# One level of Strassen's algorithm in the feed forward stages of a two-layer grid encoder

## The chip, the core and the metric
The kernel runs on one core of a Trainium2 chip as one program. The metric is the device time of one execution in microseconds. TensorE multiplies matrices, VectorE (DVE) and ScalarE (ACT) do the elementwise work, GpSimd (POOL) a part of it, and SyncE (SP) issues all the transfers of weights and activations discussed here.

## The reference
Two groups of tokens (512 prompt, 256 sample) go through the same weights, 768 tokens of width 1024 in all. Two layers, each a half-weighted feed forward, a mixer, and another half-weighted feed forward; a final norm ends it. The hidden width is 2752. The kernel's stages are therefore f, ab, f, f, c, f.
```python
def _rmsnorm(x, g):
    y = xf * lax.rsqrt(jnp.mean(xf * xf, axis=-1, keepdims=True) + NORM_EPS)
    return (y * g.astype(jnp.float32)).astype(x.dtype)
def _swiglu(h, wg, wu, wd):
    return (jax.nn.silu(h @ wg) * (h @ wu)) @ wd
...
        x = x + 0.5 * _swiglu(_rmsnorm(x, norm_ffn1[i]), ffn1_wg[i], ffn1_wu[i], ffn1_wd[i])
        h = _rmsnorm(x, norm_mix[i])
        ...
        x = x + 0.5 * _swiglu(_rmsnorm(x, norm_ffn2[i]), ffn2_wg[i], ffn2_wu[i], ffn2_wd[i])
    return _rmsnorm(x, final_norm)
```
The mixers (neighbourhood and latent attention in the first, grouped attention in the second) are not touched but for their output product.

## The kernel before
The residual stream `x` lies transposed in SBUF, 8 tiles of 128 features by 768 tokens. All products keep float32 accuracy by splitting both operands into a high part (a cast to fp32r, ScalarE) and a low part (the difference, VectorE), and by three passes: high with high, high with low, low with high. `mm3` (L163) issues these as six matmuls, one of 512 and one of 256 columns per pass.

`Weights` is a stream of weight units: SP loads a unit of 512 KB into a `raw` buffer (L149), ScalarE casts it (L161), VectorE subtracts (L162). A few units are prepared ahead of their use.

`ffn_body` walks the 21.5 hidden tiles in chunks of three (`FCH`). For a tile, `up` computes gate and up products (8 k-tiles each) into two PSUM buffers; `act` applies the row scale `rr` (1 / rms of each token, L378 and L380), silu on ScalarE (L379), the product (L388), and the split of the result (L389 on POOL, L390 on VectorE). The result stays in SBUF. `down` multiplies the chunk's activations by their rows of the down weights and adds each of the 8 output tiles to `x` (L416). Down products of one chunk stand between the up products of the next. After the last chunk each finished tile of `x` is spread into the next product's operand by `spread` (`h_hi` L247, `h_lo` L248) and squared (L258, L260). `rstd_cols` (L270 and on) and `rstd_rows` make the next norm's scale, while TensorE already works on the unscaled products. In the last feed forward `down_final` (L453) takes the final chunk a third of the tokens at a time.

Each engine executes its own list in a fixed order; the tile scheduler sets it when the program is built. `x` stays in SBUF through a whole feed forward. Before a mixer it is written to DRAM (`xscr`, L1555) and read back at its output product (L1503).

## Time and profile before
| quantity | value |
|---|---|
| time, median of 3 runs | 3011.42 us (3008.15 to 3012.95) |
| span of the profiled execution | 3010.3 us |
| PE busy | 2923.2 us, 97% |
| DVE busy | 1419.8 us, 47% |
| ACT busy | 867.8 us, 29% |
| POOL busy | 435.6 us, 14% |
| read from and written to DRAM | 218.14 MB, 55.77 MB |

The span runs from the first to the last instruction of the profiled execution. Busy time says how much of it an engine had work; it says nothing of who waited for whom. For this the chain of waits is read, which follows the last instruction back to what released it, step by step. A busy PE may still run at a lowered clock, so the granted clock of a stretch stands beside it.

### The profile page before, as it was taken

To read this page: it belongs to the slowest core of one execution; us is meant where nothing else is said; L and a number is where in the kernel's file an instruction comes from. 1 tells how busy PE (TensorE), PEld (TensorE's weight loads), DVE (VectorE), ACT (ScalarE), POOL (GpSimd) and SP (SyncE) were. 2 spreads that over 40 slices of the span, in tenths; PEclk is the share of its full clock that TensorE was granted. 3 is DMA by queue.
4 is the path that set the end of the run, shared out by engine and by line. 5 is a ranking of instruction groups with operands and counts; after the bars stand their busy time and mean duration, and the time that the engine had idled before them with its cause. 6 is when DMAs were issued, how large, how long until landed. Compare 5 with 4: busy or idle time off the path is not lost.

```text
span 3010.3 us, 42066 instructions
## 1 busy us (share of the span) xinstructions
PE 2923.2 (97%) x17562; PEld 2581.6 (86%) x17562; DVE 1419.8 (47%) x1876; ACT 867.8 (29%) x1431; POOL 435.6 (14%) x543
## 2 busy tenths in 40 slices
...
GB/s 134 64 99 93 80 63 75 83 140 255 248 241 89 71 66 62 63 62 64 77 51 62 64 64 63 63 71 88 101 117 159 129 91 63 63 64 63 64 57 50
DMA packets 314653, 276.63 MB, mean 92 GB/s; under 512 B 25888, under 2 KB 285152, under 8 KB 313440
## 3 DMA queue, kind: packets, MB, share of 16 engines
...
HBM read 218.14 MB, written 55.77 MB: 91 GB/s over the span
## 4 chain that ended last, share of the span: by engine, by line
PE 88%; DMA 5%; DVE 3%; issue 1%; ACT 1%; POOL 1%; SPq 0%; DVEq 0%; ACTq 0%; POOLq 0%
PE ps L172 73%; PE pj L525 2%; PE pj L529 2%; PE pj L528 2%; PE s L660 2%; DMA oscr<-of 1%; PE pc L918 1%; DMA mq<-mst 1%; DVE h_lo L248 1%; PE t L698 1%; PE ps L453 1%; DVE x L416 1%; PE o L720 1%; PE ps L358 1%; PE o L719 1%
## 5 line engine op out<-in xcount | busy, mean ns | idle before, releaser
L172 PE MATMUL ps<-h_hi,gul 128*128 128x512 f32 (+1 forms) x2720 | 700.4, 338 | 0.0
L172 PE MATMUL ps<-h_hi,guh 128*128 128x512 f32 (+1 forms) x2720 | 697.1, 337 | 0.0
L172 PE MATMUL ps<-h_lo,guh 128*128 128x512 f32 (+1 forms) x2720 | 696.6, 337 | 0.0
L161 ACT CAST guh<-raw 128x1024 fp32r<-128x1024 f32 (+3 forms) x224 | 232.8, 1041 | 1380.1 <-PE ps L172 1353.9
L172 PE MATMUL ps<-act,dnh 128*128 128x512 f32 (+1 forms) x2720 | 580.7, 337 | 0.0
L172 PEld LDWEIGHTS ps<-h_hi,guh 128*128 128x128 f32 x2720 | 417.2, 188 | 62.8 <-issue 0.7
L172 PEld LDWEIGHTS ps<-h_hi,gul 128*128 128x128 f32 x2720 | 416.1, 188 | 59.1
L172 PEld LDWEIGHTS ps<-h_lo,guh 128*128 128x128 f32 x2720 | 414.8, 188 | 60.2
L172 PEld LDWEIGHTS ps<-act,dnh 128*128 128x128 f32 x2720 | 416.3, 188 | 58.1
L416 DVE SCALAR_TENSOR_TENSOR x<-ps,x 128x768 f32<-128x768 f32 x248 | 234.8, 955 | 342.7 <-PE ps L172 342.6
L389 POOL TENSOR_SCALAR act<-upp 128x768 fp32r<-128x768 f32 x88 | 73.7, 837 | 1949.6 <-DVE upp L388 1639.9
L172 PE MATMUL ps<-act,dnl 128*128 128x512 f32 (+1 forms) x1296 | 331.0, 336 | 0.0
L162 DVE TENSOR_TENSOR gul<-raw,guh 128x1024 fp32r<-128x1024 f32 (+3 forms) x224 | 271.6, 1215 | 31.9 <-ACT guh L161 31.2
L380 DVE TENSOR_TENSOR upp<-ps,rr 128x768 f32<-128x768 f32 x84 | 80.4, 957 | 363.7 <-PE ps L172 363.5
L378 DVE TENSOR_TENSOR gate<-ps,rr 128x768 f32<-128x768 f32 x84 | 80.4, 958 | 300.7 <-PE ps L172 289.5
L172 PEld LDWEIGHTS ps<-act,dnl 128*128 128x128 f32 x1296 | 197.5, 188 | 27.6
L162 DVE TENSOR_TENSOR dnl<-raw,dnh 128x1024 fp32r<-128x1024 f32 x84 | 103.6, 1235 | 150.7 <-ACT dnh L161 150.7
L161 ACT CAST dnh<-raw 128x1024 fp32r<-128x1024 f32 x84 | 88.1, 1049 | 289.8 <-DMA raw<-in_ffn_wd_dram 201.8
L525 PE MATMUL pj<-guh,h_hi 128*128 128x256 f32 x576 | 168.2, 292 | 0.9 <-ACT h_hi L247 0.7
L529 PE MATMUL pj<-guh,h_lo 128*128 128x256 f32 x576 | 165.9, 288 | 0.6 <-DVE h_lo L248 0.6
L528 PE MATMUL pj<-gul,h_hi 128*128 128x256 f32 x576 | 164.8, 286 | 0.0
L646 POOL TENSOR_SCALAR p<-p,sm 128x256 f32<-128x256 f32 (+1 forms) x192 | 117.6, 625 | 138.3 <-DVE sm L643 112.2
...
## 6 DMA issues: line engine op xcount, KB each, us to landing
...
mq<-mst SPq DMA_DIRECT2D x24, 384.0 KB
...
xscr<-x SPq DMA_DIRECT2D x16, 384.0 KB
naq<-stage SPq DMA_DIRECT2D x16, 384.0 KB
```

Source lines behind the costliest of these rows:

```text
L161: nc.scalar.copy(out=h, in_=r)
L162: nc.vector.tensor_tensor(out=l, in0=r, in1=f32(h), op=ALU.subtract)
L172: mm = nc.tensor.matmul(out[:, s], w, x[:, s], start=start and n == 0, stop=stop and n == len(pairs) - 1)
L378: nc.vector.tensor_tensor(out=g, in0=pss[0][:, :T], in1=rr, op=ALU.mult)
L380: nc.vector.tensor_tensor(out=u, in0=pss[1][:, :T], in1=rr, op=ALU.mult)
L389: nc.gpsimd.tensor_scalar(out=a[:rows, 0], in0=u[:rows], scalar1=1.0, scalar2=1.0, op0=ALU.mult, op1=ALU.mult)
L416: nc.vector.scalar_tensor_tensor(out=x[:, j], in0=ps[:, :T], scalar=0.5, in1=x[:, j], op0=ALU.mult, op1=ALU.add)
L525: m = nc.tensor.matmul(out, self.h[:, k, s], wh[:, c], start=k == 0, stop=False)
L528: nc.tensor.matmul(out, self.h[:, k, s], wl[:, c], start=False, stop=False)
L529: nc.tensor.matmul(out, self.l[:, k, s], wh[:, c], start=False, stop=k == KT - 1)
L646: nc.gpsimd.tensor_scalar(out=pt[:, c], in0=pt[:, c], scalar1=sm[:, 2 + s:3 + s], scalar2=1.0, op0=ALU.mult, op1=ALU.mult)
L660: self.anchor = nc.tensor.matmul(ps[:, a:b], sa, mo, start=m == 0, stop=m == len(movs) - 1).ins
```

## The change
The feed forward is cut into two phases, and in both of them a product of two matrices, each divided into 2 by 2 blocks, is computed by seven block products for eight (Strassen's algorithm in Winograd's form, one level), with sums and differences of blocks before and after.

Up, 20 of the 21.5 hidden tiles: the stationary matrix has two rows of blocks (gate, up) and two columns (the halves of the input features, 4 k-tiles each), the moving matrix has the two halves of the features by two halves of 384 tokens (`TH`, `HALVES`). `norm_half` scales a token half of x in advance (gain and row scale in one operation) and splits it; `combine` makes the four sums t1 to t4 of x's blocks, once for a feed forward. The weight sums are made per hidden tile by four operations of 128x512 (`sums` in `plan_up`); the units of a tile are ua (gate), ud (second half of up, 512 columns), uc (the sums) and ub (up). A block product is 4 k-tiles x 3 passes = 12 matmuls of 384 columns, so a tile takes 84. The finished activations, and for each pair of tiles the four combinations of them, go to DRAM (`tq`). The tile and a half left over are computed as before, in halves.

Down: groups of four hidden tiles, 5 of them; products are taken in the order `DOWN`, all five groups of one product in a row, each group 24 matmuls. The weights come as blocks of 128x1024 (two transfers), two of the four blocks (A and C) stay in SBUF, and the block sums are made in them by VectorE. The activations of a group come back from DRAM (`plan_acts`), are cast and subtracted. x, which was written to `xscr` and released, is loaded again, and the results of a product are added to it (L640). The tile and a half left over is multiplied for the first token half (`rest(0)`) between products 7 and 3, and for the second at the end.

Also, the mixers' output product runs in token halves, so that the next feed forward's `norm_half(0)` can start before its end.
```diff
+TH = T // 2
+HALVES = (slice(0, TH), slice(TH, T))
...
+    def norm_half(self, q, ps, gain):
+        nc = self.nc
+        rr = self.rstd_rows(q, ps)
+        x = self.xn[q]
+        for j in range(KT):
+            nc.vector.scalar_tensor_tensor(out=x[:, j], in0=self.x[:, j, HALVES[q]], scalar=gain[:, j:j + 1], in1=rr,
+                                           op0=ALU.mult, op1=ALU.mult)
+            if j % 2:
+                n, m = f"b{j // 4 + 1}{q + 1}", j % 4
+                hi, lo = (t[:, m - 1:m + 1] for t in self.comb[n])
+                nc.scalar.copy(out=hi, in_=x[:, j - 1:j + 1])
+                nc.vector.tensor_tensor(out=lo, in0=x[:, j - 1:j + 1], in1=f32(hi), op=ALU.subtract)
+    def combine(self, n, out, a, b):
+        nc = self.nc
+        nc.vector.tensor_tensor(out=out, in0=a, in1=b, op=ALU.subtract)
+        hi, lo = self.comb[n]
+        nc.scalar.copy(out=hi, in_=out)
+        nc.vector.tensor_tensor(out=lo, in0=out, in1=f32(hi), op=ALU.subtract)
...
+    NS = 20
+    OPS = {1: "b11", 2: "b21", 3: "b22", 4: "t4", 5: "t1", 6: "t2", 7: "t3"}
...
+    def plan_up(self, F, t, views):
+        nc = self.nc
+        st = []
+        def sums():
+            g, u = st
+            H = 512
+            tt = nc.vector.tensor_tensor
+            tt(out=u[:, H:], in0=u[:, :H], in1=u[:, H:], op=ALU.add)
+            tt(out=u[:, :H], in0=g[:, :H], in1=u[:, :H], op=ALU.subtract)
+            tt(out=g[:, :H], in0=u[:, H:], in1=g[:, :H], op=ALU.subtract)
+            tt(out=g[:, H:], in0=g[:, H:], in1=g[:, :H], op=ALU.subtract)
+            return self.split(g)
+        def load():
+            g = self.load_weight(views[0], P, 1024)
+            if t == 0:
+                st.extend((g, self.load_weight(views[1], P, 1024)))
+                return
+            u = F.evac.tile([P, 1024], F32, tag="rawu", name="rawu", bufs=2)
+            for view, src in views[1](u):
+                nc.sync.dma_start(out=view, in_=src)
+            st.extend((g, u))
+        self.gu.entry(load, lambda _: self.split(st[0]))
+        self.gu.entry(lambda: None, lambda _: self.split(st[1][:, 512:], 512))
+        self.gu.entry(lambda: None, lambda _: sums())
+        self.gu.entry(lambda: None, lambda _: self.split(st[1]))
+    DOWN = (1, 4, 5, 2, 6, 7, 0, 3)
...
+    def load_block(self, tile, F, q, a, b):
+        for m, src in enumerate(self.down_block(F.wd, q, a, b)):
+            self.nc.sync.dma_start(out=tile[:, 512 * m:512 * m + 512], in_=src)
+        return tile
+    def plan_down(self, F, i, q):
+        nc = self.nc
+        tt = nc.vector.tensor_tensor
+        new = lambda: self.wp.tile([P, 1024], F32, tag="raw", name="raw")
+        def stash(which, a, b):
+            t = F.stash.tile([P, 1024], F32, name=f"{which}{q}")
+            getattr(F, which)[q] = self.load_block(t, F, q, a, b)
+            return t
+        def s1(raw):
+            A, C = F.A[q], F.C[q]
+            tt(out=C, in0=raw, in1=C, op=ALU.add)
+            u = self.split(C)
+            tt(out=C, in0=C, in1=A, op=ALU.subtract)
+            tt(out=A, in0=A, in1=raw, op=ALU.subtract)
+            return u
+        def s4(raw):
+            tt(out=raw, in0=raw, in1=F.C[q], op=ALU.subtract)
+            return self.split(raw)
+        if i == 1 and q < 2:
+            self.gu.entry(lambda: self.load_block(new(), F, q, 1, 1), self.split)
+        elif i == 1:
+            self.gu.entry(lambda: stash("A", 1, 1), self.split)
+        elif i == 4:
+            def load():
+                if q < 2:
+                    stash("A", 1, 1)
+                return stash("C", 2, 2)
+            self.gu.entry(load, self.split)
+        elif i == 5:
+            self.gu.entry(lambda: self.load_block(new(), F, q, 2, 1), s1)
+        elif i == 2:
+            self.gu.entry(lambda: self.load_block(new(), F, q, 1, 2), self.split)
+        elif i == 6:
+            self.gu.entry(lambda: F.C[q], self.split)
+        elif i == 7:
+            self.gu.entry(lambda: F.A[q], self.split)
+        else:
+            self.gu.entry(lambda: self.load_block(new(), F, q, 1, 2), s4)
...
+    def mm3h(self, out, wh, wl, xh, xl, start, stop, more=False):
+        nc = self.nc
+        pairs = [(wh, xh), (wh, xl)] + ([(wl, xh)] if wl is not None else [])
+        for n, (w, x) in enumerate(pairs):
+            mm = nc.tensor.matmul(out, w, x, start=start and n == 0, stop=stop and n == len(pairs) - 1, skip_group_check=more)
+        self.last_mm = mm.ins
...
+    def ffn_up(self, F, cpool, psp, gain):
...
+                    if q == 0 and i == 0 and not self.has_rc:
+                        self.rstd_cols(psum(), range(TT // 2, TT), exact=False)
+                    if q == 0 and i == 1:
+                        self.norm_half(1, psum(), gain)
...
+                    b = lambda i, j: x[j - 1][:, (lo, hi)[i - 1]]
+                    self.combine("t1", b(1, 1), b(1, 2), b(1, 1))
+                    self.combine("t3", b(1, 2), b(2, 2), b(1, 2))
+                    self.combine("t2", b(2, 2), b(2, 2), b(1, 1))
+        comb["t4"] = [cpool.tile([P, KT // 2, TH], F32R, tag=f"bt{q}", name=f"t4{q}") for q in "hl"]
+        self.combine("t4", x[0][:, hi], x[0][:, hi], x[1][:, hi])
...
+                y, b, c = psum(), psum(), psum()
+                g = ep.tile([P, T], F32, tag="g", name="g", bufs=2)
+                act = ep.tile([P, 2, TH], F32, tag="act", name="act", bufs=3)
+                ua = self.gu.get(2)
+                product(1, ua, 0, y)
+                a1 = copy(y, "a1")
+                ud = self.gu.get(2)
+                product(2, ua, 512, b)
+                tt(out=g[:, :TH], in0=b[:, :TH], in1=a1, op=ALU.add)
+                uc = self.gu.get(2)
+                product(6, uc, 0, y, False)
+                u2 = copy(y, "u2")
+                ub = self.gu.get(2)
+                product(5, ub, 512, c)
+                p5 = copy(c, "p5")
+                product(7, ub, 0, y, False)
+                c22 = ep.tile([P, TH], F32, tag="c22", name="c22", bufs=2)
+                tt(out=c22, in0=y[:, :TH], in1=p5, op=ALU.add)
+                product(3, uc, 512, c, False)
+                tt(out=g[:, TH:], in0=c[:, :TH], in1=u2, op=ALU.add)
+                nc.scalar.activation(out=g, in_=g, func=AF.Silu)
+                product(4, ud, 0, y, False)
+                tt(out=act[:, 0], in0=y[:, :TH], in1=g[:, :TH], op=ALU.mult)
+                tt(out=act[:, 1], in0=c22, in1=g[:, TH:], op=ALU.mult)
+                q, m = t // 4, t // 2 % 2
+                if t % 2 == 0:
+                    nc.sync.dma_start(out=F.tq[q][0][:, m], in_=act[:, 0])
+                    prev = act
+                    continue
+                tl = ep.tile([P, 4, TH], F32, tag="tl", name="tl", bufs=2)
+                tt(out=tl[:, 0], in0=prev[:, 1], in1=prev[:, 0], op=ALU.subtract)
+                tt(out=tl[:, 1], in0=act[:, 1], in1=tl[:, 0], op=ALU.subtract)
+                tt(out=tl[:, 2], in0=act[:, 1], in1=prev[:, 1], op=ALU.subtract)
+                tt(out=tl[:, 3], in0=act[:, 0], in1=tl[:, 1], op=ALU.subtract)
+                nc.sync.dma_start(out=F.tq[q][1:3, :, m].rearrange("i p c -> p i c"), in_=act)
+                nc.sync.dma_start(out=F.tq[q][3:7, :, m].rearrange("i p c -> p i c"), in_=tl)
...
+    ADDS = {1: [(0, 0)], 4: [(1, 0)], 5: [(1, 1), (0, 1)], 2: [(0, 0)], 6: [(0, 1)], 7: [(1, 1), (1, 0)], 3: [(0, 1)]}
...
+        for j in range(KT):
+            nc.sync.dma_start(out=x[:, j], in_=self.xscr[j])
...
+        def product(i, banks, first):
+            for q in range(NQ):
+                (wh, wl), (th, tl) = gu.get(2), tu.get(1)
+                for j in range(4):
+                    out = banks[j // 2][:, j % 2 * 512:j % 2 * 512 + TH]
+                    for m in range(2):
+                        w, c = slice(512 * m + P * j, 512 * m + P * j + P), slice(TH * m, TH * m + TH)
+                        self.mm3h(out, wh[:, w], wl[:, w], th[:, c], tl[:, c], first and q + m == 0, q + m == NQ, not first)
+                yield q
+            for b, ps in enumerate(banks):
+                for r, c in self.ADDS[i]:
+                    add(ps, [4 * r + 2 * b, 4 * r + 2 * b + 1], HALVES[c])
...
+        chain = [new("y") for _ in range(2)]
+        for i in self.DOWN:
+            if i == 0:
+                rest(0)
+                continue
+            banks = chain if i in (1, 6, 7) else [new("y" if i == 3 else "x") for _ in range(2)]
+            for q in product(i, banks, i not in (6, 7)):
+                if i == 3:
+                    if final is not None and q > 0 and q < 4:
+                        final(q - 1, new("x"))
+                    elif after is not None:
+                        after(q, lambda: new("x"))
+                elif jobs and q == 4:
+                    jobs.pop(0)(misc)
+        rest(1)
```
What stood in the old `FCH`, `up`, `act`, `down` and `down_final` is removed.

The order of the work moves with it. On VectorE in the middle of feed forward 1's up work, before: gate and up scale, the low parts of two units (gul, dnl), the product with silu.
```order
L378 TENSOR_TENSOR gate_2291<-ps_2192,rr_105 128x768
L162 TENSOR_TENSOR gul_2302<-raw_2299,guh_2301 128x1024
L380 TENSOR_TENSOR upp_2292<-ps_2241,rr_105 128x768
L162 TENSOR_TENSOR gul_2308<-raw_2305,guh_2307 128x1024
L388 TENSOR_TENSOR upp_2292<-upp_2292,gate_2291 128x768
L390 TENSOR_TENSOR act_2290<-upp_2292,act_2290 128x768
L162 TENSOR_TENSOR dnl_2554<-raw_2551,dnh_2553 128x1024
L378 TENSOR_TENSOR gate_2410<-ps_2311,rr_105 128x768
L162 TENSOR_TENSOR gul_2435<-raw_2432,guh_2434 128x1024
```

On VectorE at the same place after, one hidden tile from product 7 on: raw and rawu are the gate and up weights, gul the low parts, c22 and g the sums of products.
```order
L567 TENSOR_TENSOR c22_2754<-ps_2658,p5_2740 128x384
L168 TENSOR_TENSOR gul_2725<-rawu_2704,guh_2724 128x512
L382 TENSOR_TENSOR rawu_2704<-rawu_2704 128x512
L383 TENSOR_TENSOR rawu_2704<-raw_2702,rawu_2704 128x512
L384 TENSOR_TENSOR raw_2702<-rawu_2704,raw_2702 128x512
L385 TENSOR_TENSOR raw_2702<-raw_2702 128x512
L569 TENSOR_TENSOR g_2661<-ps_2660,u2_2722 128x384
L168 TENSOR_TENSOR gul_2795<-raw_2702,guh_2794 128x1024
L572 TENSOR_TENSOR act_2662<-ps_2658,g_2661 128x384
L573 TENSOR_TENSOR act_2662<-c22_2754,g_2661 128x384
L168 TENSOR_TENSOR gul_2813<-rawu_2704,guh_2812 128x1024
L558 TENSOR_TENSOR g_2788<-ps_2786,a1_2810 128x384
```

Four weight sums and the low part of uc (gul_2795) now stand between the result of product 7 (c22) and the activations, and product 6 of the next tile reads gul_2795.

On VectorE at the start of feed forward 1, before: the diagonals of the row scale and low parts of weights.
```order
L286 CAST rh_439<-rc_75 128x6
L287 TENSOR_TENSOR rl_440<-rc_75,rh_439 128x6
L291 TENSOR_TENSOR diag_443<-ident_60,rh_439 128x768
L162 TENSOR_TENSOR gul_399<-raw_277,guh_398 128x1024
L162 TENSOR_TENSOR gul_405<-raw_402,guh_404 128x1024
L162 TENSOR_TENSOR dnl_546<-raw_543,dnh_545 128x1024
L378 TENSOR_TENSOR gate_453<-ps_299,rr_105 128x768
L380 TENSOR_TENSOR upp_454<-ps_300,rr_105 128x768
```

After, behind the eight scalings of the second token half: low parts of x's blocks (b12l, b22l), the combinations (L290) and their low parts (t1l, t3l), and the leftover tile's activation between them.
```order
L285 TENSOR_TENSOR b12l_337<-x_133,b12h_336 128x768
L290 TENSOR_TENSOR xn_135<-x_133,xn_135 128x1536
L285 TENSOR_TENSOR b12l_337<-x_133,b12h_336 128x768
L285 TENSOR_TENSOR b22l_329<-x_133,b22h_328 128x768
L522 COPY ru2_457<-ps_425 64x384
L285 TENSOR_TENSOR b22l_329<-x_133,b22h_328 128x768
L290 TENSOR_TENSOR x_133<-x_133 128x4x384
L293 TENSOR_TENSOR t1l_331<-xn_135,t1h_330 128x1536
L168 TENSOR_TENSOR gul_580<-raw_318,guh_579 128x512
L524 TENSOR_TENSOR ract2_456<-rg2_455,ru2_457 64x384
L290 TENSOR_TENSOR x_133<-x_133,xn_135 128x4x384
L293 TENSOR_TENSOR t3l_335<-x_133,t3h_334 128x1536
```

The first weight units of tile 0 (gul_580, and the sums further on) stand behind this work.

On SP, before, a feed forward issued only loads of weights, here in its middle.
```order
L149 DMA raw_3086<-in_ffn1_wd_dram 128x1024
L149 DMA raw_3092<-in_ffn1_wd_dram 128x1024
L149 DMA raw_3098<-in_ffn1_wd_dram 128x1024
L149 DMA raw_3264<-in_ffn1_wg_dram 128x8x128
L149 DMA raw_3270<-in_ffn1_wu_dram 128x8x128
```

After, where up turns into down in feed forward 1: traw is an activation operand read back, C1 and C2 are stationary blocks.
```order
L596 DMA traw_3341<-tq0_4_83 128x768
L634 DMA x_3192<-xscr0_115 128x768
L634 DMA x_3192<-xscr1_116 128x768
L634 DMA x_3192<-xscr2_117 128x768
L634 DMA x_3192<-xscr3_118 128x768
L634 DMA x_3192<-xscr4_119 128x768
L634 DMA x_3192<-xscr5_120 128x768
L634 DMA x_3192<-xscr6_121 128x768
L634 DMA x_3192<-xscr7_122 128x768
L410 DMA C1_3374<-in_ffn1_wd_dram 128x512
L410 DMA C2_3431<-in_ffn1_wd_dram 128x512
L596 DMA traw_3381<-tq0_0_79 128x768
```

traw_3381, the first operand of product 4, is issued behind the eight loads of x and two half blocks.

## Rows read from the trace of the kernel before
**Rows 1.** The page, its parts 1 (busy us by engine) and 2 (40 slices).
```profile
PE 2923.2 (97%) x17562; PEld 2581.6 (86%) x17562; DVE 1419.8 (47%) x1876; ACT 867.8 (29%) x1431; POOL 435.6 (14%) x543
...
GB/s 134 64 99 93 80 63 75 83 140 255 248 241 89 71 66 62 63 62 64 77 51 62 64 64 63 63 71 88 101 117 159 129 91 63 63 64 63 64 57 50
```

**Rows 2.** The chain of waits in order: start us, us, what.
```profile
22.88 11.17 PE ps L358 x47
...
43.35 506.82 PE ps L172 x2902
...
572.74 0.84 ACT ssh L269
573.61 0.97 DVE ssl L270
...
1010.89 512.41 PE ps L172 x2927
...
1584.66 485.90 PE ps L172 x2774
...
2298.38 10.96 DMA gq<-gq
...
2314.56 5.50 DMA osum<-oscr
...
2492.51 475.15 PE ps L172 x2720
```

**Rows 3.** The timeline of PE at 632 us: start us, us, engine, line, operation.
```profile
632.25 0.46 PE L882 MATMUL tq<-identr,hl 128*128 128x128 f32 x4
...
633.14 0.33 PE L1245 MATMUL pq<-guh,cth 128*128 128x384 f32 x1
...
633.66 0.33 PE L1245 MATMUL pq<-guh,cth 128*128 128x384 f32 x1
```

**Rows 4.** Groups of DVE by line and form: busy us, mean ns, idle before.
```profile
L162 DVE TENSOR_TENSOR gul<-raw,guh 128x1024 fp32r<-128x1024 f32 x214 | 262.2, 1227 | 14.4 <-ACT guh L161 13.7
L416 DVE SCALAR_TENSOR_TENSOR x<-ps,x 128x768 f32<-128x768 f32 x248 | 234.8, 955 | 342.7 <-PE ps L172 342.6
...
L705 DVE TENSOR_TENSOR ptl<-t,pth 128x512 fp32r<-128x512 f32 x144 | 96.2, 681 | 28.3 <-ACT pth L704 27.9
...
L1218 DVE TENSOR_TENSOR ctl<-gc,cth 128x384 fp32r<-128x384 f32 x6 | 3.3, 555 | 0.8 <-ACT cth L1217 0.6
```

**Rows 5.** The same groups of ACT.
```profile
L161 ACT CAST guh<-raw 128x1024 fp32r<-128x1024 f32 x214 | 224.4, 1051 | 1354.6 <-PE ps L172 1330.5 <-PE pj L529 14.1 <-issue 4.6
...
L379 ACT ACTIVATE gate<-gate 128x768 f32<-128x768 f32 x84 | 71.2, 848 | 50.3 <-DVE gate L378 50.3
```

**Rows 6.** Windows: us, busy us of PE to POOL, PEclk, DMA share, GB/s.
```profile
572.00:574.00 2.00, 1.41 (x9) 1.04 (x7) 1.10 (x2) 0.83 (x1) 0.00 (x0) 1.00 0.33 89
574.00:576.00 2.00, 1.38 (x11) 1.30 (x11) 0.57 (x1) 0.00 (x0) 0.00 (x0) 1.00 0.45 150
576.00:578.00 2.00, 1.74 (x7) 1.74 (x7) 0.17 (x1) 0.33 (x1) 1.35 (x1) 0.54 0.06 20
578.00:580.00 2.00, 2.00 (x10) 2.00 (x9) 0.00 (x0) 0.64 (x2) 0.00 (x0) 0.61 0.00 0
1546.00:1548.00 2.00, 0.81 (x6) 0.49 (x5) 1.10 (x2) 0.83 (x1) 0.00 (x0) 1.00 0.72 252
1548.00:1550.00 2.00, 2.00 (x16) 1.72 (x15) 0.97 (x2) 1.05 (x1) 0.00 (x0) 1.00 0.00 0
```

**Rows 7.** Windows with the highest transfer rates, columns as in rows 6.
```profile
850.00:860.00 10.00, 9.31 (x53) 8.51 (x52) 6.67 (x15) 5.94 (x17) 3.38 (x6) 0.70 1.04 370
930.00:940.00 10.00, 10.00 (x59) 8.74 (x58) 0.00 (x0) 0.00 (x0) 0.48 (x1) 1.00 0.78 287
```

**Rows 8.** The transfers issued: tensors, queue, kind, count, KB each.
```profile
gq<-gq SPq DMA_DIRECT2D x16, 384.0 KB
osum<-oscr SPq DMA_DIRECT2D x8, 768.0 KB
```

517 lines of the change are left out of this document (275 added, 242 removed).

## Prediction
> **What bounds the kernel now.** I read the page's first two parts, then the chain of waits, then the groups by operation, then short windows around the ends of the feed forwards. TensorE is busy 97% of the span, VectorE 47% [rows 1]. The chain of waits spends four unbroken stretches on line 172, one per feed forward: 506.82 us with 2,902 matmuls, 512.41 with 2,927, 485.90 with 2,774, 475.15 with 2,720 [rows 2]. That is 0.175 us per matmul in each of them, for a mean of 384 columns (the lengths alternate 512 and 256). Nothing else is late in there: TensorE's issue is the bound, and the number of matmuls is what the time is made of. Matmuls of 384 columns exist in this trace and start 0.173 us apart (633.14 to 633.66 in three steps), so cutting the columns in another way costs nothing by itself [rows 3].
>
> **What it removes.** Before, a feed forward has 43 gate and up units of 8 k-tiles × 3 passes × 2 pieces and a down product of the same make, 3,104 matmuls. After, it has 20 tiles × 84 in the up phase, 144 for the tile and a half left over, 7 × 5 × 24 = 840 down and 80 for the rest: 2,744. The 360 fewer, four times, are 1,440 × 0.174 = **-250.6 us**. The last feed forward's last rest runs as 120 matmuls of 128 columns; four of that width start within 0.29 us [rows 3], so 120 × 0.0725 = 8.7 instead of 40 × 0.174 = 7.0: **+1.7**. TensorE would be no longer the bound only where another engine has more work than this leaves it, and that is what the rest of the sum goes through.
>
> Of the matmul's price the Trainium skill has a rule: its page "TensorE: Matmul & The Clock Gate", section "Back-to-back issue gap", gives N/2.4 + 2.5 ns at full clock for an isolated matmul, 162.5 ns for 384 columns. The rows have 173 to 175 ns; by the rule the saving would be 234 us and every time below 17 us later, and I keep the rows.
>
> **VectorE in the up loop.** Per hidden tile TensorE has 84 × 0.174 = 14.6 us. VectorE has three splits of 128x1024 (1.227 each), one of 128x512 and four weight sums of that size (0.68, from the nearest 128x512 row), and seven operations of 384 columns (0.555): 3.68 + 3.40 + 3.89 = 11.0 us, 75% [rows 4]. In all it fits, but it works in a fixed order. The chain that counts begins when product 7 of a tile ends: c22 0.555, the low part of ud 0.68, four sums 2.72, then g for product 3 (which ended 23 matmuls after 7, at 4.0) 0.555, silu 0.85, cast of the sums 1.05, their low part 1.23 [rows 4, 5]. With 4.0 as the start of g this is 7.7 us, and some 0.1 to 0.5 for five hand-overs (the rows at 572 to 574 show 0.03 each between VectorE and ScalarE [rows 2]; an answer from TensorE takes longer). The cover is 44 matmuls until product 6 of the next tile, plus its first two, which use high parts only: 46 × 0.174 = 8.0 us. A wait of 0 to 0.4 us on each of 80 tiles: 0 to +32; I take 0.15, **+12**.
>
> **Stage starts.** Before, the gain alone was multiplied in ahead and the row scale came with the activation. Now VectorE has to scale the second half's x (8 × 0.555), split it (4 × 0.955), build three combinations of 128x1536 that are needed first and split them (6 × 1.77, from the slope of the 768 and 1024 rows), finish the leftover activations (some 3 us), and make tile 0's sums and low parts (5.2), with the two diagonals 28 us in all. From the point at which the second half's scale is known TensorE has 24 + 72 + 24 matmuls, 21 us, until product 6 of tile 0. The wait is 7 us if all of it falls in that window; the scheduler puts a little behind it, and I take 6.3. A break of TensorE can cost clock too: after two breaks of together 1.2 us at 572 to 576 the granted clock was 0.54 and 0.61 in the next two windows of 2 us, a loss of 1.7 us; after one break of 1.2 us at 1546 it stayed at 1.00 [rows 6]. I take 1.7 for a break this long: 4 × 8.0 = **+32**, with bounds 12 and 40. In the first feed forward the first product also waits for a normalised half of x, that is for three token tiles, their statistics, 8 scalings and 4 splits, where before TensorE ran unbroken from 22.88 [rows 2]; 8 × 0.555 + 4 × 0.955 and two diagonals make about **+10.5**.
>
> **From up to down.** Activations go out to DRAM and come back, x is reloaded, and the stationary blocks A and C come in, all on SP's one queue. Product 1 runs from blocks and activations fetched before; it covers 5 × 24 × 0.174 = 20.9 us. Product 4's first operand is a load issued behind 26 other transfers: blocks A2 to A4, the last combinations going out, three and a half more blocks, one load of activations, eight of x and two half blocks, some 8.65 MB since the up phase's buffers came free. The best rates in the trace are 370 GB/s over 10 us, and 287 at a share of 0.78, 368 at full share [rows 7]: 23 to 25 us, 2 us until the first can go, a cast of 0.83 and a landing of 1 to 2: 27 to 29. Wait 6.3 (bounds 0 and 9), with clock 8: 4 × 8 = **+32**. That a load waits behind others shows in part in the chain: a copy of 384 KB took 10.96 us where 768 KB elsewhere took 5.50 [rows 2, 8].
>
> The Trainium skill, page "DMA: Bandwidth & Descriptors", section "Queues, rings and completion order", states that each DMA engine consumes a queue's descriptors in ring order; by it the whole 8.65 MB counts as I count it. If a later load could overtake, this term would be 0 and the sum 32 us lower; no run here shows that.
>
> **Down phase.** Between products 4 and 5, 5 and 2, 6 and 7 the next product writes the bank that VectorE has just to empty (two adds of 128x768, 0.955 each, behind splits): 1 + 1 + 1 us, 4 × 3 = **+12**. Products 4 and 5 need 37 us of VectorE (five splits of weights and of activations, ten sums and differences of 1024 columns) beside 42 us of TensorE: +2 each, **+8** (0 to 20). The rest between products 7 and 3 finds four adds (3.8 us), a difference and two low parts (3.0) ahead of its second operand on VectorE, while TensorE has three matmuls to do; where a mixer follows, eight h_lo of 0.555 and four adds stand before product 3's operand as well. 8 us in feed forwards 1 and 3, 4 in 2 and 4: **+24** (12 to 40). Ends: +1 each for the shorter last groups, **+4**; the final part leaves earlier by about 2: **-2**. Given back are before's own breaks, which sit at 572 to 580 and at the other mixer, 2.9 us each, and the break of 1.2 us at three starts [rows 6]: **-10**.
>
> **Sum.** -250.6 + 1.7 + 12 + 32 + 10.5 + 32 + 12 + 8 + 24 + 4 - 2 - 10 = -126.4. The profiled execution has a span of 3010.3 us, 1.1 below the median of the runs; 3010.3 - 126.4 + 1.1 = **2885 us**.
>
> **Rivals.**
> *Covers hold.* Every wait but the first start is hidden, since a stall of TensorE also lets VectorE catch up and the stalls above overlap. -250.6 + 1.7 + 10.5 + 12 (starts at their lower bound) + 4 - 12 = -234: 2777. For it speaks VectorE's 75%; against it the fixed order. Chance 0.17.
> *The down phase is bound by transfers.* It moves some 35 MB per feed forward (27 blocks of 0.52 MB, 36 activations of 0.39, x in and out) in 920 × 0.174 = 160 us, 219 GB/s, where most slices before ran at 60 to 140 [rows 1]. Short stretches have seen 370 [rows 7]; but if strided blocks and DRAM round trips give only 195, it lasts 180 us, +20 four times: 2960. Chance 0.11.
> *Slower: the up loop waits on every tile and the clock falls with it.* If the chain from product 7 to product 6 overruns its cover by 0.6 us and each such break is followed by the clock loss at 576 to 580 (1.7 us), a tile costs 2.3 us: 80 × 2.3 = 184 in place of 12, 3057. It decides the sign from 1.73 us per tile on, (126 + 12)/80. Against it: the break at 1546, alone in its surroundings, cost no clock [rows 6]. Chance 0.07.
> *No change.* The change does not shorten TensorE's work, or all losses add up to the gain. TensorE's order has the fewer matmuls in it, so it takes a coincidence: 0.02.
>
> **How the numbers follow.** The forecast with all its bounds (2813 to 2952: 72 us of waits that may be missing, 67 that may be added) has 0.63. The range should leave out 2 in 10: from 2795, which takes in most of the overlap case, to 2962, which takes in the transfer case. A measurement of this kernel can tell about 0.2%, 6 us, from no change. Faster by more than that: 0.63 + 0.17 + 0.11 = 0.91; within: 0.02; slower: 0.07.
>
> **What would show it.** Right: 84 matmuls of a tile in about 14.8 us with a break under 0.4 us ahead of product 6 and the clock at 1.00; a break of 5 to 8 us ahead of product 6 of tile 0, one of like size at the first matmul of product 4 released by a load, and one at the leftover product between 7 and 3 released by VectorE; matmuls of 384 columns 0.174 apart. The overlap case would show those breaks under 2 us; the transfer case, breaks at most blocks of the down phase released by loads, with a DMA share near 1; the slow case, a granted clock below 0.9 through the up loops. The prediction is wrong from its base if matmuls of 384 columns with a fresh stationary operand each do not keep 0.174 us for long.

## The result, and the profile after

The change made the kernel slower: 3049.08 us (median of 4 runs, 3044.68 to 3056.32) against 3012.18 us before (4 runs, 3008.15 to 3015.6), a ratio of 1.0129 with a 95% interval of 1.011 to 1.0148. The span of the profiled execution grew from 3010.3 to 3051.0 us. The forecast was 2885 us.

First the page of after, part 1 (busy us by engine).
```profile
PE 2767.8 (91%) x16118; PEld 2665.3 (87%) x16118; DVE 1980.5 (65%) x2850; ACT 1303.8 (43%) x2118; POOL 372.5 (12%) x488
```
TensorE works 155 us less than in [rows 1], and waits 196 us more: its share fell from 97% to 91%. VectorE has 561 us more to do. The price of a matmul of 384 columns held. Here are three rows of the timeline of PE in a hidden tile of the second feed forward (start us, us, engine, line, operation):
```profile
1112.26 0.34 PE L465 MATMUL ps<-t4h,guh 128*128 128x384 f32 x1
...
1113.67 0.34 PE L465 MATMUL ps<-t4h,gul 128*128 128x384 f32 x1
...
1114.35 0.44 PE L465 MATMUL ps<-t2h,guh 128*128 128x384 f32 x1 [0.34 <-ACT guh L167]
```
From 1112.26 to 1113.67 there are eight steps, 0.176 us each, as in [rows 3]. So the 1,440 matmuls less are worth their 250 us, and the rest of the document is about what ate them.

For that I lay every matmul of a feed forward in its piece (leftover, tiles, products, rests) and count what the steps from one matmul's end to the next one's take beyond 0.1743 us (0.0725 for 128 columns). The breaks are in it, and the slow matmuls behind a break. The forecast's terms stand beside the pieces that they belong to. Sums over the four feed forwards, in us. "Combined" is the experiment c1_all_four below:

```
piece                        forecast  after  e1_sums_first  combined
leftover tiles at the start       -     17.5      16.8          16.7
tile 0                           32     48.6      49.3          28.7
tiles 1 to 5                   \ 12     48.1      15.0          17.0
tiles 6 to 19                  /        17.8      11.2          11.2
products 1 and 4                 32     52.7      53.5          36.7
products 5, 2, 6, 7              20     31.9      31.6          29.5
first rest and product 3         24     54.7      53.8          21.9
second rest                       4     16.0      14.7          14.3
all                             124    287       246           176
```
Before, the same count gives 22.5 us (12,416 matmuls in 2,186.6 us of feed forward). The two sides of the result fit: -250.6 + 1.7 + 287 - 22.5 + 13.8 (the first feed forward starts at 36.7 us instead of 22.9) + 11 (the stretches between and behind the feed forwards, almost all of it the first mixer) = +40.4, against +40.7 in the spans.

The largest single break is that of **tile 0**, four times. VectorE and TensorE in the second feed forward (timeline, as above; x8 is a run of eight instructions):
```profile
1050.04 4.29 DVE L279 SCALAR_TENSOR_TENSOR x<-x,g_norm_ffn,ps 128x384 f32<-128x384 f32 x8 [1.28 <-PE ps L327]
...
1066.79 1.75 DVE L293 TENSOR_TENSOR t3l<-x,t3h 128x1536 fp32r<-128x1536 f32 x1
1068.45 0.68 DVE L383 TENSOR_TENSOR raw<-raw 128x512 f32<-128x512 f32 x1
...
1069.64 1.75 DVE L290 TENSOR_TENSOR x<-x 128x1536 f32<-128x1536 f32 x1
1071.30 1.75 DVE L293 TENSOR_TENSOR t2l<-x,t2h 128x1536 fp32r<-128x1536 f32 x1
...
1074.29 1.75 DVE L293 TENSOR_TENSOR t4l<-x,t4h 128x1536 fp32r<-128x1536 f32 x1
...
1076.42 0.68 DVE L385 TENSOR_TENSOR raw<-raw 128x512 f32<-128x512 f32 x1
...
1079.18 0.69 PE L465 MATMUL ps<-t1h,guh 128*128 128x384 f32 x1 [9.70 <-ACT guh L167]
```
From 1050.04 to 1077.1 VectorE has no hole. The last of the four weight sums (L385) stands at its end, with work on t2, t3 and t4 between the sums; t3 and t4 are asked for by products 7 and 4 alone, later than the sums. Behind it ScalarE makes two casts of 1.04 us until the first matmul can go. TensorE started its last matmul at 1069.15 and stands still for 9.7 us.

In **tiles 1 to 5** each tile lost 2.4 us. From tile 6 on the mean is 0.3, all of it in tiles 6 (1.1) and 8 (2.3); from tile 9 on nothing is lost. Here are ScalarE, VectorE and TensorE ahead of tile 2, which is of the first kind, and ScalarE and TensorE ahead of tile 7, which is of the second:
```profile
1111.07 0.85 ACT L570 ACTIVATE g<-g 128x768 f32<-128x768 f32 x1 [2.35 <-DVE g L569]
1113.24 1.05 ACT L167 CAST guh<-raw 128x1024 fp32r<-128x1024 f32 x1 [1.33 <-DVE raw L385]
...
1112.00 0.56 DVE L558 TENSOR_TENSOR g<-ps,a 128x384 f32<-128x384 f32 x1 [0.36 <-ACT g L570]
1112.47 0.68 DVE L385 TENSOR_TENSOR raw<-raw 128x512 f32<-128x512 f32 x1
...
1105.40 0.33 PE L465 MATMUL ps<-b11l,guh 128*128 128x384 f32 x1
1105.58 0.34 PE L465 MATMUL ps<-t3h,guh 128*128 128x384 f32 x1
...
1194.88 1.05 ACT L167 CAST guh<-raw 128x1024 fp32r<-128x1024 f32 x1 [1.98 <-DVE raw L385]
1195.83 0.84 ACT L570 ACTIVATE g<-g 128x768 f32<-128x768 f32 x1
...
1190.45 0.34 PE L465 MATMUL ps<-b11h,gul 128*128 128x384 f32 x1
```
Same work, other order, on three engines. At 1111 silu stands before the cast of the next tile's weight sums, and VectorE's last sum (L385) waits its turn behind operations around silu (L558); at 1194 the cast goes first. On TensorE, ahead of tile 2, nearly all of the next tile's product 1 (b11) is done when product 7 (t3) begins; ahead of tile 7 most of it follows product 7, which began at 1188.34. So between product 7 and product 6 of the next tile (t2, at 1114.35) TensorE has 31 to 37 matmuls of cover ahead of tiles 1 to 6, and 44 from tile 7 on. Silu stands first ahead of tiles 1 to 6 and 8 and nowhere else, in all four feed forwards. Ahead of tile 8 the cover is 44, but the cast of a first activation of the down phase comes in between.

At **product 4** the load of its first activations is late, at the **first rest** a low part on VectorE. PE, SP and VectorE, second feed forward:
```profile
1407.85 0.33 SPq L596 DMA_DIRECT2D traw<-tq  x1
...
1415.68 1.01 PE L465 MATMUL x<-th,guh 128*128 128x384 f32 x2 [4.99 <-ACT th L607]
1417.55 0.69 PE L465 MATMUL x<-tl,guh 128*128 128x384 f32 x1 [0.86 <-DVE tl L608]
1418.04 0.52 PE L465 MATMUL x<-th,gul 128*128 128x384 f32 x1
...
1531.01 3.54 DVE L640 SCALAR_TENSOR_TENSOR x<-y,x 128x768 f32<-128x768 f32 x4
1534.47 1.21 DVE L168 TENSOR_TENSOR gul<-raw,guh 128x1024 fp32r<-128x1024 f32 x1
1535.60 0.55 DVE L608 TENSOR_TENSOR tl<-traw,th 128x384 fp32r<-128x384 f32 x1
...
1536.20 0.69 PE L465 MATMUL x<-tl,guh 128*128 128x384 f32 x1 [2.94 <-DVE tl L608]
```
The windows there, and one behind tile 0's break (columns as in [rows 6]), show a DMA share near 1 before and in product 4's break (1.04 and 1.03) and half the clock behind both breaks (0.50, the 1.2 GHz level):
```profile
1390.00:1402.00 12.00, 11.27 (x63) 10.63 (x61) 5.30 (x5) 4.96 (x6) 0.00 (x0) 1.00 1.04 381
...
1408.00:1414.00 6.00, 2.68 (x16) 2.36 (x14) 1.92 (x2) 0.94 (x1) 0.00 (x0) 0.89 1.03 396
1414.00:1420.00 6.00, 3.46 (x10) 2.95 (x11) 5.83 (x6) 3.76 (x5) 0.00 (x0) 0.50 0.78 279
...
1079.00:1085.00 6.00, 5.82 (x17) 5.38 (x18) 3.27 (x4) 1.45 (x3) 0.00 (x0) 0.50 1.14 300
```

### The profile page after: what moved, and what is told of

Same layout as the page of the kernel before. It is cut to its first block, busy times and chain, and to the rows that moved or that the text cites. A ratio compares the mean times of both kernels' runs of the same rounds, so it can differ in the third digit from the quotient of the medians.

```text
span 3051.0 us, 42088 instructions
## 1 busy us (share of the span) xinstructions
PE 2767.8 (91%) x16118; PEld 2665.3 (87%) x16118; DVE 1980.5 (65%) x2850; ACT 1303.8 (43%) x2118; POOL 372.5 (12%) x488
## 3 DMA queue, kind: packets, MB, share of 16 engines
q1 hardware_dynamic: 414112, 433.63, 46.4%
## 5 line engine op out<-in xcount | busy, mean ns | idle before, releaser
L465 PE MATMUL x<-th,guh 128*128 128x384 f32 (+1 forms) x640 | 214.2, 354 | 50.6 <-ACT th L607 39.6
L465 PE MATMUL x<-tl,guh 128*128 128x384 f32 (+1 forms) x640 | 223.8, 354 | 21.8 <-DVE tl L608 21.8
L465 PE MATMUL y<-tl,guh 128*128 128x384 f32 x640 | 220.2, 344 | 13.2 <-DVE tl L608 13.2
L465 PE MATMUL y<-th,gul 128*128 128x384 f32 x640 | 218.1, 341 | 0.0
L465 PE MATMUL y<-th,guh 128*128 128x384 f32 x640 | 208.1, 341 | 7.0 <-ACT th L607 6.7
L465 PE MATMUL x<-th,gul 128*128 128x384 f32 (+1 forms) x560 | 194.2, 347 | 0.0
L465 PEld LDWEIGHTS x<-th,guh 128*128 128x128 f32 x640 | 127.0, 202 | 58.8 <-ACT th L607 47.0
L608 DVE TENSOR_TENSOR tl<-traw,th 128x768 fp32r<-128x768 f32 (+1 forms) x156 | 145.1, 932 | 50.1 <-ACT th L607 49.9
L465 PEld LDWEIGHTS x<-tl,guh 128*128 128x128 f32 x640 | 129.1, 202 | 29.2 <-DVE tl L608 29.1
L168 DVE TENSOR_TENSOR gul<-rawu,guh 128x512 fp32r<-128x512 f32 (+1 forms) x152 | 144.3, 949 | 0.0
```

Source lines behind the costliest of these rows:

```text
L168: nc.vector.tensor_tensor(out=l, in0=r, in1=f32(h), op=ALU.subtract)
L465: mm = nc.tensor.matmul(out, w, x, start=start and n == 0, stop=stop and n == len(pairs) - 1, skip_group_check=more)
L608: nc.vector.tensor_tensor(out=tl[:, :n], in0=t[:, :n], in1=f32(th[:, :n]), op=ALU.subtract)
```

## The experiments

Theory: the loss is many waits, each at a place where something stands too early in a fixed order (on ScalarE, VectorE or a ring), so each can be taken away alone. Rivals: VectorE is simply short, so that a wait taken away comes back next door; the lost clock is a cost of its own; seven products for eight do not pay in the down phase.

### Sums first in the up loop: e1_sums_first
```diff
-            tt(out=g[:, H:], in0=g[:, H:], in1=g[:, :H], op=ALU.subtract)
-            return self.split(g)
+            F.summed = tt(out=g[:, H:], in0=g[:, H:], in1=g[:, :H], op=ALU.subtract)
+            u = self.split(g)
+            F.cast = self.cast
+            return u
...
+                self.tc.add_manual_dep(glo.ins, F.summed.ins.name, NOSYNC, reason="sums first")
...
-                ub = self.gu.get(2)
+                ub = self.gu.get(3 if t < self.NS - 1 else 2)
...
+                self.tc.add_manual_dep(silu.ins, F.cast.ins.name, NOSYNC, reason="sums first")
```


> Edit: in the up loop ScalarE casts the next tile's weight sums before the silu of this tile, and VectorE makes all four sums before it takes the gate result of the next tile, in every tile; in the changed kernel this is so from tile 6 on only. Nothing is left out. Theory (order): the 48 us that tiles 1 to 5 lose in the four feed forwards (12.2, 12.5, 11.3, 12.1) come from that order; they fall to under 10, and the time to about 3005 to 3015. Rival (load): VectorE is behind after the stage's start and the tiles have to wait until it has caught up, whatever the order; the loss of tiles 1 to 5 stays above 35 and the time above 3035.

3010.57 us (10 runs, 3002.53 to 3021.33), ratio to before 1.0003 (0.9988 to 1.0018). Tiles 1 to 5 lose 15.0 us (under 10 was expected) where they lost 48.1, tiles 6 to 19 11.2 for 17.8, and nothing else in the table moved by more than 2 us. Order alone, with not one operation taken away, was worth 38.5 us. Which engine's order it was the run does not separate: with these pins TensorE's cover is 44 matmuls too, from tile 2 on. ScalarE in tile 1 of this kernel:
```profile
1082.81 1.05 ACT L167 CAST guh<-raw 128x1024 fp32r<-128x1024 f32 x1 [4.37 <-DVE raw L385]
1083.76 0.84 ACT L573 ACTIVATE g<-g 128x768 f32<-128x768 f32 x1
```

### Eight products in the down phase: e2_down_by_eight
The down phase of after with eight block products, without weight sums and without combinations of activations; the up phase is left as it is.
```diff
-    DOWN = (1, 4, 5, 2, 6, 7, 0, 3)
+    DOWN = ((0, 0), (0, 1), 0, (1, 0), (1, 1))
...
-        F.tq = [self.dram.tile([7, P, 2, TH], F32, name=f"tq{n}_{q}") for q in range(self.NS // 4)]
+        F.tq = [self.dram.tile([4, P, 2, TH], F32, name=f"tq{n}_{q}") for q in range(self.NS // 4)]
```


> Edit: one part undone. The up phase keeps its seven products, the down phase takes all eight block products of each quadrant (120 matmuls more per feed forward, 480 in all, +84 us), without block sums, without stationary blocks that stay, and without combinations of the activations; activations still go through DRAM, and x is still loaded again. Nothing is left out. Theory (VectorE and the queue of loads together make the down phase's 157 us of breaks): without sums, with 4 block loads less in front and a first product twice as long, the breaks fall to about 50; 3049 + 84 - 107 = 3026, between 3010 and 3045. Rival (the round trip of activations and x through DRAM is what costs): the breaks stay above 120 and the time is above 3090.

3121.35 us, ratio 1.0367 (1.0347 to 1.0386): 72 us slower than after. The 480 matmuls more are 83.7 us; the down phase's losses fell from 155 to 89 us, so that part alone comes to +17. The rest came mostly from the up loop, whose code is the same: tiles 6 to 19 lost 81 us instead of 18, tiles 1 to 5 32 instead of 48 (some 8 us I could not place; the two profiled executions are 67.6 us apart and leave 4). With other work behind it the scheduler put silu before the cast in 19 of the 20 tiles of each feed forward, and left 35 matmuls of cover, or 31, ahead of every tile:
```profile
1191.27 0.85 ACT L529 ACTIVATE g<-g 128x768 f32<-128x768 f32 x1 [2.36 <-DVE g L528]
1193.44 1.05 ACT L167 CAST guh<-raw 128x1024 fp32r<-128x1024 f32 x1 [1.32 <-DVE raw L387]
```
The time lies in the rival's range, but for this other reason: the breaks came to neither the 50 us of the theory nor the rival's 120. So seven for eight in the down phase pays, but little (17 of 84 us) as long as its waits stay; and the run shows the price of that order a second time, 1.5 us per tile.

### x loaded by need: e3_x_by_need
```diff
-        for j in range(KT):
-            nc.sync.dma_start(out=x[:, j], in_=self.xscr[j])
+        def load(js, q):
+            for j in js:
+                self.after_product(nc.sync.dma_start(out=x[:, j, HALVES[q]], in_=self.xscr[j][:, HALVES[q]]))
...
+                if (i, q) in ((1, 1), (4, 1), (4, 3), (5, 0)):
+                    load(*{(1, 1): (range(4), 0), (4, 1): (range(4, KT), 0), (4, 3): (range(4, KT), 1), (5, 0): (range(4), 1)}[i, q])
```


> Edit: x is loaded in quarters, each a product ahead of its use (0.79 MB instead of 3.15 MB stand before the first activation load of product 4). Nothing is left out. Theory (queue): the break ahead of product 4 (46 us of loss over four feed forwards with its lowered clock) falls to under 15 and the time to 3010 to 3022. Rival (volume): the blocks A and C, the activations and the weights alone keep the queue full for as long; the loss stays above 35, the time above 3038.

3042.83 us, ratio 1.0104 (1.0087 to 1.0121). Product 4 kept 43.6 of its 46.2 us:
```profile
1403.36 0.62 PE L465 MATMUL x<-th,guh 128*128 128x384 f32 x2 [1.89 <-ACT th L607]
1407.99 0.69 PE L465 MATMUL x<-tl,guh 128*128 128x384 f32 x1 [4.01 <-DVE tl L608]
```
The wait for the load is 3.1 us shorter, and the low part is 3.2 us later behind it. Less was taken away than the edit says: 2.4 MB of x no longer stand ahead of that load, but SP's list has four half blocks of C (1 MB) more there. The rival's figures came (over 35 us, over 3038); its mechanism, a queue full for as long, did not. VectorE has sums for product 5 (L425) ahead of the operand of product 4:
```profile
1403.58 1.22 DVE L425 TENSOR_TENSOR C<-raw,C 128x1024 f32<-128x1024 f32 x1
1404.71 1.22 DVE L168 TENSOR_TENSOR gul<-C,guh 128x1024 fp32r<-128x1024 f32 x1
1405.85 1.22 DVE L425 TENSOR_TENSOR C<-raw,C 128x1024 f32<-128x1024 f32 x1
1406.98 1.82 DVE L608 TENSOR_TENSOR tl<-traw,th 128x768 fp32r<-128x768 f32 x2
```
Taken alone this speaks for either: a VectorE that is short, or one that does the wrong thing first.

### The first rest a product earlier: e4_rest_earlier
```diff
-    DOWN = (1, 4, 5, 2, 6, 7, 0, 3)
+    DOWN = (1, 4, 5, 2, 6, 0, 7, 3)
```
The work of the next norm that went with the rest goes behind product 7.

> Edit: the leftover tile and a half of the first token half is multiplied between products 6 and 7 instead of between 7 and 3; the work on finished x of that half follows product 7. Nothing is left out. Theory (order): its second operand then does not stand behind the four adds of product 7 and its adds not before product 3's operand; the loss at the leftover and at product 3 (26 + 28 us) falls to 15 to 25 together, the time to 3015 to 3025. Rival (load): VectorE has the same work around the end of product 7, and the loss moves to product 7 or 3; the time stays above 3038.

3047.51 us, ratio 1.0114 (1.0094 to 1.0133). The rest's own loss fell to 10.2 us in all, and product 7 rose to 24.2, product 3 kept 19.2 of 28.3, the last second rest rose to 13.7 from 7.2. A moved step takes its queue with it.

### The breaks filled: e5_filled_breaks
```diff
+    def warm(self, ps, n):
+        for _ in range(n):
+            mm = self.nc.tensor.matmul(ps[:, :P], self.onesr, self.identr, start=True, stop=True)
...
+                if t == 0:
+                    self.warm(c, 110)
```


> The kernel e1_sums_first with idle matmuls (128 columns, operands that are never rewritten, into a bank that the next product overwrites) put ahead of the five breaks of each FFN: 110 before product 6 of the first tile, 60 before product 4, 12 before 5, 30 before the first rest, 25 before 3; at 0.0725 us each 17.2 us per FFN, against breaks of 9.7, 5.9, 1.9, 2.6 and 3.3 us (23 us) in e1_sums_first. Theory: a part of the loss at each break is the granted clock of half after it; its records show 75 us of clock lost in the four FFNs of e1_sums_first, some 60 of it behind these breaks. Then the lost clock falls below 30 us and the time from 3010.6 to 2950 to 2975. Rival: the half clock in the records hides no time that the break itself would not have cost, and the fillers only lengthen what they stand in: 3005 to 3030, whatever the clock says.

3005.97 us, ratio 0.9983 (0.9971 to 0.9995), 4.6 us under e1_sums_first with intervals that overlap. Timeline and a window:
```profile
1053.67 11.17 PE L473 MATMUL ps<-identr,onesr 128*128 128x128 f32 x99
1064.67 0.39 PE L467 MATMUL ps<-t1h,guh 128*128 128x384 f32 x1
...
1062.00:1068.00 6.00, 6.00 (x45) 6.00 (x45) 2.94 (x4) 1.12 (x2) 0.00 (x0) 1.00 0.94 259
```
The clock did stay at 1.00 where the other kernels show 0.50, and tile 0's half clock is gone. In all four feed forwards the clock that the records show as lost fell from 75 to 27 us, as the theory wanted, and the time did not follow. The fillers were too long. In the second feed forward the scheduler set 11 of the 110 elsewhere; the other 99 hold TensorE from 1053.67 to 1064.67, 0.11 us each and not 0.0725, which is 1.3 longer than the break, and tile 0 still lost 45.6 us for 49.3. All fillers together took 27 us per feed forward, for 17 planned and breaks of 23. Nor were the 75 us all there to be won: some 24 of them lie in time in which TensorE had nothing to do. What costs is the slow matmuls behind a break: 18 in 6.1 us at tile 0 of after (1079.18 to 1085.25) where 3.1 would do, 2.9 us; 17 in 5.3 at product 4 (1417.55 to 1422.84), 2.3 us; by a count of all such steps some 36 us over the four feed forwards of e1_sums_first, and 18 with the fillers. So the theory's time is refuted, and the rival's came at the lower end of its range. What fillers of the right length would bring is not shown; the slow matmuls bound it.

### Tile 0's order: e7_first_tile
```diff
-                    self.combine("t3", b(1, 2), b(2, 2), b(1, 2))
-                    self.combine("t2", b(2, 2), b(2, 2), b(1, 1))
+                    self.combine("t2", b(1, 1), b(2, 2), b(1, 1))
+        self.gu.prefetch(3)
+        self.combine("t3", b(1, 2), b(2, 2), b(1, 2), F.summed)
...
-        self.combine("t4", x[0][:, hi], x[0][:, hi], x[1][:, hi])
+        self.combine("t4", x[0][:, hi], x[0][:, hi], b(1, 1), F.summed)
```
The last argument is an instruction that must stand ahead. The second half's norm also starts four k-tiles earlier; the two are not separated.

> The kernel e1_sums_first with another order on VectorE at the start of the up phase: the second half's norm a few matmuls earlier, t2 before t3 and t4, and the weight sums of tile 0 ahead of t3 and t4, which products 2 and 5 or later ask for. Theory: the break of 9.7 us before product 6 of the first tile is a queue on one engine (VectorE is busy without a hole there and the sums of the weights stand last in it), so that the break falls to 1 to 4 us, the first tile's loss from 49 us over the four FFNs to 15 to 25, and the time from 3010.6 to 2975 to 2990. Rival: the engine is simply short of time for everything that the first tile asks for, and the break reappears before the product that asks for t3 or t4: first tile's loss over 40 us, time 3000 to 3012.

2989.91 us, ratio 0.9926 (0.9906 to 0.9945), 20.7 us under e1_sums_first, at the upper end of what was expected. Tile 0 loses 28.2 us for 49.3 (15 to 25 was expected): the break is now one of 1.04 us and one of 3.33, since t3's and t4's differences and t2's low part still stand before the low part of the sums:
```profile
1052.92 0.44 PE L469 MATMUL ps<-t1h,guh 128*128 128x384 f32 x1 [1.04 <-ACT guh L167]
...
1058.17 0.69 PE L469 MATMUL ps<-t1h,gul 128*128 128x384 f32 x1 [3.33 <-DVE gul L168]
```

### Two loads moved at product 4: e8_later_loads
The edit of e3_x_by_need on e1_sums_first, and:
```diff
             def load():
-                if q < 2:
-                    stash("A", 1, 1)
-                return stash("C", 2, 2)
+                c = stash("C", 2, 2)
+                if q > 2:
+                    t = F.stash.tile([P, 1024], F32, name=f"A{q - 3}")
+                    F.A[q - 3] = self.load_block(t, F, q - 3, 1, 1)
+                return c
```


> The kernel e1_sums_first with the loads at the start of the down phase spread out: the residual stream (3.1 MB) in four parts between product 1 and product 5, and the two weight blocks that product 4 loads a second time (1 MB) in its last two steps. Theory: product 4's first break is a load that waits behind others on the rings (DMA share 1.02 to 1.04 there), so with 4.1 MB out of its way product 4's loss over the four FFNs falls from 46.4 us to below 25 and the time to 2980 to 2995. Rival, from e3_x_by_need, where the load came 3 us sooner and VectorE's cast came 3 us later: VectorE's queue sets it as much as the load, product 4 keeps 35 us or more, time 3000 to 3011.

2996.48 us, ratio 0.9947 (0.9928 to 0.9966), 14.1 us under e1_sums_first, 1.5 above what was expected. Product 4 loses 24.4 us for 46.4, product 1 12.3 for 7.1:
```profile
1383.44 0.62 PE L469 MATMUL x<-th,guh 128*128 128x384 f32 x2 [1.69 <-ACT th L613]
1384.83 0.44 PE L469 MATMUL x<-tl,guh 128*128 128x384 f32 x1 [0.77 <-DVE tl L614]
```
VectorE comes to the low parts straight after one low part of a block; the sums for product 5 no longer stand there:
```profile
1382.68 1.22 DVE L168 TENSOR_TENSOR gul<-C,guh 128x1024 fp32r<-128x1024 f32 x1
1383.82 1.82 DVE L614 TENSOR_TENSOR tl<-traw,th 128x768 fp32r<-128x768 f32 x2
```
So in e3_x_by_need VectorE was not short of time, it had product 5's sums first. Moving the blocks that those sums need moved the sums as well: the wait for the load is much as in e3_x_by_need (1.69 and 1.89), the one for the low part fell from 4.01 to 0.77. Of the 22 us that went at product 4, 5 came back at product 1.

### The rests prepared ahead: e9_rest_ahead
```diff
+            w, tag = (T, "t") if n == T else (TH, "r")
+            th = ring.tile([P, w], F32R, tag=tag + "h", name=tag + "h", bufs=2)
...
+                if q == NQ - 2 and i in (7, 3):
+                    gu.prefetch(3)
+                    tu.prefetch(3)
```


> The kernel e1_sums_first with the casts for both rests taken ahead: own buffers for the rest's activations, loaded and cast during the last step of products 7 and 3, and the rest's second weight tile a step earlier, so that they stand on VectorE ahead of the adds of the product just ended. Theory: the breaks at the first rest, at product 3 and at the second rest are casts queued behind adds on one engine that need not be there; rest, 3 and second rest lose 68.5 us in e1_sums_first, of it some 20 us of idle time and 18 of clock at the rests themselves; they fall to 30 to 40 and the time to 2975 to 2990. Rival, from e4_rest_earlier, where the loss moved with the order: VectorE has no room there, the casts taken ahead push the adds back and product 3 or 7 waits for its bank instead: 60 us or more remain, time 3003 to 3012.

2976.66 us, ratio 0.9888 (0.9865 to 0.9911), 33.9 us under e1_sums_first. First rest, product 3 and second rest lose 35.6 us for 68.5, and in the second feed forward the first rest has no break over 0.5 us. VectorE there:
```profile
1486.99 0.55 DVE L613 TENSOR_TENSOR rl<-traw,rh 128x384 fp32r<-128x384 f32 x1
...
1490.57 1.81 DVE L645 SCALAR_TENSOR_TENSOR x<-y,x 128x768 f32<-128x768 f32 x2
1492.30 0.55 DVE L613 TENSOR_TENSOR rl<-traw,rh 128x384 fp32r<-128x384 f32 x1
```
Against e4_rest_earlier this is the difference between moving a queue and putting two short low parts further forward in it, one ahead of the four adds and one between them.

### All four: c1_all_four
The edits of e7_first_tile, e8_later_loads and e9_rest_ahead on e1_sums_first.

> e1_sums_first with the edits of e7_first_tile, e8_later_loads and e9_rest_ahead together. Theory (each loss is a place of its own, a queue or a ring in which something stands too early): the gains add, 3010.6 - 20.7 - 14.1 - 33.9 = 2942, within 2935 to 2950, and the four FFNs lose some 175 us against a gapless 0.1743 us per matmul (245 in e1_sums_first). Rival (one engine, VectorE, is short in the down phase, so that what one edit frees the next needs again): 2955 to 2975, with the losses of products 4, 5 and 3 higher than in the single runs.

2939.07 us (2937.59 to 2940.71), ratio 0.9757 (0.9742 to 0.9771). The gains add to within 3 us, and the table's losses come to 176 us where 175 were expected. The rival of a short VectorE has fallen for these waits: it is 67% busy here and 76% in the down phase of the second feed forward, and the gains added. In what is left, tile 0's 28.7 us for one, it is not tested.

### The bias tables: c2_jobs_later and c3_tables_up
What remained in the first feed forward were breaks of 6.1 and 5.8 us in products 4 and 5, released by loads, in stretches like this (windows of c1_all_four):
```profile
400.00:412.00 12.00, 9.66 (x56) 9.34 (x54) 5.77 (x5) 2.84 (x3) 0.00 (x0) 1.00 0.98 204
...
428.00:440.00 12.00, 6.98 (x39) 6.34 (x37) 8.79 (x8) 1.05 (x1) 0.00 (x0) 0.99 0.98 222
```
The DMA share is 0.98 at 204 to 222 GB/s, where it was 1.04 at 381 with loads of weight blocks and x (1390 to 1402 us of after). In there are these (DMA issues of c1_all_four):
```profile
nbd_s<-nb SPq DMA_DIRECT2D x1, 2032.0 KB
nbd_p<-nb SPq DMA_DIRECT2D x1, 2016.0 KB
```
c2_jobs_later puts the jobs into products that load no weights:
```diff
-                elif jobs and q == 4:
+                elif jobs and q == 1 and i in (2, 6, 7):
```


> c1_all_four with the three table jobs of the first FFN (two bias tables, one rope table) put into products 2, 6 and 7, of which the last two load no weights, and not into 1, 4 and 5. Theory: the first FFN's breaks of 7.0 and 5.5 us in products 4 and 5 (e8_later_loads: two stretches in which the DMA share is 0.95 to 1.05 at 190 to 240 GB/s, the rows of a table being written in small pieces) are these jobs; they go, and the time falls by 9 to 13 us under c1_all_four, to about 2931. Rival: the tables take as long wherever they are written and the activations of products 6 and 7 then wait instead: within 4 us of c1_all_four.

2943.59 us, ratio 0.977 (0.9748 to 0.9793), no gain on c1_all_four. In the first feed forward products 4 and 5 lost 6.4 us for 22.1, products 6 and 7 18.4 for 0.6: the rival. c3_tables_up writes the two bias tables in tiles 8 and 12 of the up phase:
```diff
+                if len(jobs) > 1 and t in (8, 12):
+                    jobs.pop(0)(misc)
```


> c1_all_four with the two bias tables of the first FFN written in its up phase (tiles 8 and 12), where a tile of 14.6 us loads 1 MB, and only the rope table left in the down phase. Theory: in c2_jobs_later the same two jobs cost products 6 and 7 breaks of 7.6 and 5.7 us, as they cost products 4 and 5 in c1_all_four; they cost whatever asks the rings for its activations next, and in the up phase nothing asks for as much: 2939.1 less 10 to 14, 2925 to 2929. Rival: the weights of the tiles behind them are late by as much as the activations were, or the job disturbs the order on ScalarE that e1_sums_first mended: 2935 to 2950.

2928.14 us (5 runs, 2922.4 to 2933.23), ratio 0.9722 (0.9706 to 0.9738). The first feed forward loses 35.0 us for 47.2, as the theory said. This is the fastest kernel here: 82 us below the runs of before beside it, 121 below the change as it was made.

## Why the prediction was wrong

The gain was right, and most places of the waits were named rightly; the sign was lost in their sizes. Term by term, forecast and measured:

- **The removed matmuls**, -250.6: right. 0.174 to 0.176 us per matmul of 384 columns held through all four feed forwards. The formula for an isolated matmul in the Trainium skill ("TensorE: Matmul & The Clock Gate", section "Back-to-back issue gap") gives 162.5 ns, which is again not what the rows show.
- **The up loop**, +12: the step that failed most, 65.9. What failed first is the cover. I counted 44 matmuls between product 7 and product 6 of the next tile, and two more; that is so from tile 7 on, but ahead of tiles 1 to 6 the scheduler had drawn the next tile's product 1 in front of product 7, and 31 to 37 were left, with the two more 5.8 to 6.8 us and not 8.0. The chain of 7.7 us failed too, by less: ahead of tile 2 it took 8.3 (1107.96 to 1116.28), because four operations on activations stand ahead of the low part (1113.07 to 1115.07). The tile whose list I had read, and took for all 20, is of the good kind. Where silu stood first (28 tiles) a tile lost some 2.2 us, about the price in the slower rival, without that rival's mechanism: the granted clock was 0.99 from 1086 to 1236 us and 1.00 from there to 1386. That the time came out near this rival's 3057 is chance; its loop would have lost 184 us. e1_sums_first shows that order is the cause: 38.5 us came back.
- **Tile 0**, +32: 48.6. VectorE's 28 us were matched by luck (27.1 without a hole): the two operations for t4 stand in it, 3.5 us which the sum left out, and the low parts of the weight sums, which it counted, come behind. I took 6.3 us for the wait and it was 9.7, since ScalarE's two casts behind the last sum (2.1 us with the hand-over) were in no term and TensorE's cover from the start of VectorE's work was 19.4 us, not 21; behind it stood 2.9 of clock for 1.7. The upper bound of 40 did not hold it either.
- **First start**, +10.5: 13.8.
- **Product 4's load**, +32: 52.7 with product 1. A wait of 5.0 and 0.9 us where I had 6.3, with 2.3 of clock, was near in three feed forwards; the first lost 18.4 us there and 10.0 in product 5. I left out that feed forward's bias tables: their 2 MB writes share the rings (c3_tables_up shows 12 us). That a load waits for what is ahead of it fits e3_x_by_need, where some 1.3 MB less ahead of it made its wait 3.1 us shorter. The Trainium skill ("DMA: Bandwidth & Descriptors", section "Queues, rings and completion order") states that each DMA engine consumes descriptors in ring order, and this run agrees with it.
- **Banks, products 4 and 5**, +20: 31.9, of which the tables explain some.
- **Rest and product 3**, +24: 54.7, beyond its bound of 40. The queue on VectorE was named rightly, yet the sum charged only the idle time there. It left out the half clock behind two or three breaks of 2 to 3 us in a row (19 us of lost clock in the records of after, part of it a cost), and that product 3's low part waits once more. e9_rest_ahead took 32 us of it away.
- **Second rest, leftover start**, +4: 33.5. Breaks of 2.3 us at the second rest's low part (in the second feed forward) and 2.5 us at the first low part of a feed forward behind a mixer were in no term. The term of +1.7 for the last rest was mis-sized as well: a run of its 128-column matmuls starts 0.112 us apart (29 steps from 3026.96 to 3030.20, granted clock 1.00), where four in a row had given 0.0725, so that the 120 of them cost +6.4.
- **Given back**, -10: -22.5.
- **Mixers**, in no term: +11, of which 10.9 in the first. No run shows why.

Together this is some 165 us, and only what is given back came out better than its value. Most waits were priced from the operations needed and the cover as the program text has them; what the scheduler puts between the former, or takes out of the latter, goes on top, so such errors have one sign. The range treated them as independent and two-sided. Two of its sums are off without weight here: the transfer rival's four times 20 us come to 2965, not 2960, and by the terms' own lower bounds 84 us of waits could have been missing, not 72. Of the rivals, "covers hold" and "transfer-bound" are refuted: the breaks are there, and the DMA share near 1 is a matter of short stretches (start of the down phase, tables): in the second feed forward it is 1.01 at 375 GB/s from 1388 to 1414 us and 0.50 at 155 from there to 1588. What c3_tables_up leaves (168 us of losses) still keeps the kernel 43 us above the forecast.
